# One hybrid decoder layer on one core: the first three-part product of each column block in 512 columns instead of twice 256

## The chip, the core and the metric

The kernel runs on one core of a Trainium2 chip. The metric is the device time of one execution in microseconds (us). The kernel before takes 1066.27 us, the median of three runs (1066.21, 1066.27 and 1082.69). The profile comes from a fourth execution, which took 1077.18 us. A difference of less than 2% (21.3 us of the median) is treated as no difference.

## The reference, cut to what matters

The layer has 512 tokens of width 1024 and works in float32. Three sub-layers follow each other: a SwiGLU feed-forward network (FFN), a mixer (a gated convolution beside a sparse attention), and a second FFN. Each is preceded by a norm and added to the residual stream.

```
h = modulate(rmsnorm(x))
x = x + 0.5 * gt1 * (silu(h @ w1_gate) * (h @ w1_up)) @ w1_down     # 1024 -> 2816 -> 1024
x = x + gt2 * mixer(h)        # one input projection, attention, one output projection
x = x + 0.5 * gt3 * (silu(h @ w2_gate) * (h @ w2_up)) @ w2_down
out = rmsnorm(x) * g_final
```

Nearly all arithmetic is in these matrix products. Everything is held transposed: channels lie on the 128 partitions, the 512 tokens are the columns.

## The kernel before, in words

**Three-part products.** TensorE multiplies in a 32-bit form of less precision than float32, so each float32 operand is split into a high and a low part (`whi`, `wlo` for weights; `hhi`, `hlo` for the normed input; `ghi`, `glo` for the FFN's hidden values). One product of a 128x128 weight tile with 128x512 values is made as three: high weight by high value, high weight by low value, low weight by high value. The helper `mm3` (line 280) issues them. Each matmul first loads its 128x128 weight tile (LDWEIGHTS) and then streams the columns of values (MATMUL). Where the product is 512 columns wide, `mm3` cuts it into the two halves of `HALVES`, and issues the three parts for the left half, then the three for the right: six weight loads and six matmuls of 256 columns. Both halves add up in one 128x512 bank of PSUM, of which there are eight.

**Column blocks.** A column block is one 128x512 output tile that is summed over all its input tiles in one bank, in one go on TensorE. `start` is true at its first input tile, `stop` at its last.

- `project` (line 542) makes one block from the 8 tiles of `h`. The FFN's `main` calls it twice (gate and up) for 19 of the 22 hidden tiles of each FFN; the mixer's `fill` calls it for 14 blocks.
- `part` (line 616) makes one block of the FFN's down projection from 11 hidden tiles. `main` calls it 8 times for the first half of the hidden tiles and 8 times for the second; of the latter the last two blocks are made in separate 256-column halves.
- `output` (line 1650) makes the mixer's output projection from 8 tiles: five blocks side by side, a sixth alone, and the last two in separate halves.

The other three hidden tiles of each FFN and the mixer's first six blocks are made by `first_products` and `first_group`, which start with a 256-column half, because the operands of the two halves become ready at different times.

**Order of the work.** All instructions are written out in straight line. A planner (class `Plan`) simulates the five engines with fixed costs for every operation and so decides the order in which the instructions are put into each engine's queue. A three-part product of 512 columns has the cost `c_mm3(512)`, whatever number of instructions it is made of. Weights come by DMA in units of 512 KB; ScalarE (ACT) rounds them to `whi` (line 372) and VectorE (DVE) or GpSimd (POOL) makes `wlo` (line 361). The two last units of the first FFN and of the mixer are kept in tiles of their own (`whik`, `wlok`, and `PT`).

Of the kernel before, what the change touches and what calls it, by code (L numbers as in the profile page):

```python
# [255 lines left out]
def tile_hymba_layer(ctx: ExitStack, tc: tile.TileContext, xT, pos, cols_d, con_d, wa0, wa1, f1a, f1b, f1d,  # L256
# [9 lines left out]
    HALVES = (slice(0, T // 2), slice(T // 2, T))  # L266
# [10 lines left out]
    def mm(o, lhsT, rhs, start, stop):  # L277
        nc.tensor.matmul(o, lhsT, rhs, start=start, stop=stop)  # L278

    def mm3(o, w, x_, start, stop):  # L280

        n = o.shape[-1]
        wide = n == T and x_[0].shape[-1] == T
        halves = HALVES if wide else (slice(0, n),)
        for ts in halves:
            x0, x1 = (x_[0][:, ts], x_[1][:, ts]) if wide else x_
            o_ = o[:, ts] if wide else o
            mm(o_, w[0], x0, start and ts is halves[0], False)
            mm(o_, w[0], x1, False, False)
            mm(o_, w[1], x0, False, stop and ts is halves[-1])  # L290
# [251 lines left out]
    def project(b):  # L542

        u = take_unit()
        yield made[u]
        for d in range(DK):
            yield c_mm3(T)
            mm3(bank_of[b], cols(u, d), h_of(d), d == 0, d == DK - 1)
        free_unit(u)
# [17 lines left out]
    def first_group(order, built, accs, end, n_cols=2 * GRP):  # L567

        uses = {}
        for n, (i, d) in enumerate(order):  # L570
            yield built[i, d]
            if d not in uses:
                uses[d] = take_unit()
            yield made[uses[d]]
            ts = HALVES[i]
            for j in range(n_cols):
                if n == 0:
                    accs[j] = yield banks
                yield c_mm3(T // 2)
                mm3(bank_of[accs[j]][:, ts], cols(uses[d], j), h_of(d, ts), n == 0, n == len(order) - 1)  # L580
            if i == 1:
                free_unit(uses[d])
        done(end)


    def ffn(s, gp, accs, norm, end):
# [30 lines left out]
        def part(half, d, b, ts, keep=False):  # L617
            for k in range(FH):
                n = d * FH + k
                if (half, n // 8) not in at:  # L620
                    at[half, n // 8] = take_unit()
                u = at[half, n // 8]
                yield made[u]
                yield g_in[half * FH + k]
                yield c_mm3(ts.stop - ts.start)
                mm3(bank_of[b][:, ts], cols(u, n % 8), (ghi[k][:, ts], glo[k][:, ts]), k == 0, k == FH - 1)
                if n % 8 == 7 and not keep:
                    free_unit(u)
                if half == 0 and d == DK - 1:
                    give(gs[k], k)  # L630
# [38 lines left out]
    start = ctx.enter_context(ExitStack())  # L669
# [298 lines left out]
    with ExitStack() as mixer:  # L968
# [634 lines left out]
        n = 0  # L1603
# [295 lines left out]
```

## Time and profile before

| what | value |
|---|---|
| three runs | 1066.21, 1066.27, 1082.69 us |
| median | 1066.27 us |
| the profiled execution | 1077.18 us |
| its span, first to last instruction | 1075.4 us |
| TensorE (PE) busy | 1054.2 us, 98% |
| weight loads (PEld) busy | 1009.8 us, 94% |
| VectorE (DVE), ScalarE (ACT), GpSimd (POOL) busy | 606.0, 408.7, 51.2 us |
| matmuls, and as many weight loads | 8753 |
| mean granted TensorE clock | 0.991 of full speed |

The profiled execution has 1.8 us around its span. Matmuls are pipelined: the recorded duration of one (about 0.28 us for 256 columns) is longer than the time until the next one starts, so the busy share of TensorE says little, and the spacing of the starts tells how fast it works. A number of matmuls divided into a stretch in which TensorE does nothing else gives that spacing.

### The profile page before, as it was taken

To read this page: it belongs to the slowest core of one execution; us is meant where nothing else is said; L and a number is where in the kernel's file an instruction comes from. 1 tells how busy PE (TensorE), PEld (TensorE's weight loads), DVE (VectorE), ACT (ScalarE), POOL (GpSimd) and SP (SyncE) were. 2 spreads that over 40 slices of the span, in tenths; PEclk is the share of its full clock that TensorE was granted. 3 is DMA by queue.
4 is the path that set the end of the run, shared out by engine and by line. 5 is a ranking of instruction groups with operands and counts; after the bars stand their busy time and mean duration, and the time that the engine had idled before them with its cause. 6 is when DMAs were issued, how large, how long until landed. Compare 5 with 4: busy or idle time off the path is not lost.

```text
span 1075.4 us, 20561 instructions
## 1 busy us (share of the span) xinstructions
PE 1054.2 (98%) x8753; PEld 1009.8 (94%) x8753; DVE 606.0 (56%) x1069; ACT 408.7 (38%) x713; POOL 51.2 (5%) x47
## 2 busy tenths in 40 slices
PE   8999999999999999999999999999999999999997
PEld 5899999999999999998887789999999999999997
DVE  4988888833333347699787786744333333233334
ACT  4552222222222224458566775333222122222321
POOL 0310100000000001021001010000000000000000
PEclk8999999999999999999999999999999999999999
DMA  9669999422232231344201014133233322322202
GB/s 336 250 217 324 326 322 323 150 99 99 99 99 99 93 89 48 122 125 160 80 18 37 1 29 130 45 118 118 83 95 99 98 84 94 99 99 85 93 21 79
DMA packets 40732, 134.02 MB, mean 125 GB/s; under 512 B 4704, under 2 KB 8032, under 8 KB 40000
## 3 DMA queue, kind: packets, MB, share of 16 engines
q1 hardware_dynamic: 40640, 132.71, 37.0%
q8 instruction: 68, 1.11, 0.4%
q14 instruction: 24, 0.20, 0.1%
HBM read 130.14 MB, written 2.10 MB: 123 GB/s over the span
## 4 chain that ended last, share of the span: by engine, by line
PE 80%; DVE 10%; DMA 6%; issue 2%; ACT 1%; SPq 0%; DVEq 0%; ACTq 0%
PE b L278 77%; DMA araw<-in_wa_dram 6%; DVE ada L871 3%; PE b L1402 2%; DVE wlo L361 2%; DVE afirst L742 1%; DMA wfirst<-in_wa_dram 1%; DVE glo L613 1%; DVE s L525 1%; ACT whi L372 0%; PE b L1297 0%; DVE s L1045 0%; DVE s L606 0%; DVE swp L1048 0%; DVE afirst L739 0%
## 5 line engine op out<-in xcount | busy, mean ns | idle before, releaser
L278 PE MATMUL b<-hhi,whi 128*128 128x256 f32 x1824 | 515.8, 283 | 0.0
L278 PE MATMUL b<-hlo,whi 128*128 128x256 f32 x1824 | 509.2, 279 | 0.6 <-DVE hlo L531 0.6
L278 PE MATMUL b<-hhi,wlo 128*128 128x256 f32 x1824 | 508.7, 279 | 0.0
L372 ACT ACTIVATE whi<-raw 128x1024 fp32r<-128x1024 f32 (+3 forms) x176 | 178.2, 1013 | 461.4 <-issue 250.3
L278 PEld LDWEIGHTS b<-hhi,whi 128*128 128x128 f32 x1824 | 343.3, 188 | 7.6 <-issue 6.7
L278 PEld LDWEIGHTS b<-hlo,whi 128*128 128x128 f32 x1824 | 346.5, 190 | 1.1 <-DVE hlo L531 1.0
L278 PEld LDWEIGHTS b<-hhi,wlo 128*128 128x128 f32 x1824 | 343.5, 188 | 0.0
L361 DVE TENSOR_TENSOR wlo<-raw,whi 128x1024 fp32r<-128x1024 f32 (+3 forms) x162 | 191.1, 1180 | 223.8 <-ACT whi L372 223.5
L278 PE MATMUL b<-ghi,whi 128*128 128x256 f32 x672 | 188.0, 280 | 0.0
L278 PE MATMUL b<-ghi,wlo 128*128 128x256 f32 x672 | 187.3, 279 | 0.0
L278 PE MATMUL b<-glo,whi 128*128 128x256 f32 x672 | 187.3, 279 | 0.0
L278 PEld LDWEIGHTS b<-glo,whi 128*128 128x128 f32 x672 | 127.6, 190 | 0.0
L278 PEld LDWEIGHTS b<-ghi,whi 128*128 128x128 f32 x672 | 126.2, 188 | 0.8 <-issue 0.8
L278 PEld LDWEIGHTS b<-ghi,wlo 128*128 128x128 f32 x672 | 126.3, 188 | 0.0
L606 DVE TENSOR_TENSOR s<-sg,b 128x512 f32<-128x512 f32 x44 | 30.0, 685 | 102.1 <-PE b L278 101.4
L871 DVE SCALAR_TENSOR_TENSOR ada<-araw,cact,ada 128x1024 f32<-128x1024 f32 x49 | 63.5, 1296 | 16.8 <-DMA araw<-in_wa_dram 16.2
L361 POOL TENSOR_TENSOR wlo<-raw,whi 128x768 fp32r<-128x768 f32 (+2 forms) x14 | 32.2, 2299 | 213.5 <-ACT whi L372 213.5
L538 DVE SCALAR_TENSOR_TENSOR x<-b,mod,x 128x512 f32<-128x512 f32 (+1 forms) x30 | 19.1, 643 | 40.8 <-PE b L278 40.7
L456 ACT ACTIVATE s<-x 128x256 f32<-128x256 f32 (+1 forms) x41 | 19.4, 491 | 54.8 <-DVE x L538 52.8
L611 ACT ACTIVATE ghi<-s 128x512 fp32r<-128x512 f32 x44 | 27.1, 620 | 15.5 <-DVE s L606 15.5
L529 ACT ACTIVATE hhi<-s,mod 128x256 fp32r<-128x256 f32 (+1 forms) x42 | 20.9, 534 | 31.2 <-DVE s L525 25.6
L613 DVE TENSOR_TENSOR glo<-s,ghi 128x512 fp32r<-128x512 f32 x44 | 32.1, 734 | 0.0
(238 smaller groups left out, 963.7 us busy)
## 6 DMA issues: line engine op xcount, KB each, us to landing
araw<-in_wa_dram SPq DMA_DIRECT2D x56, 512.0 KB
raw<-in_f1b_dram SPq DMA_DIRECT2D x38, 512.0 KB
raw<-in_f2b_dram SPq DMA_DIRECT2D x38, 512.0 KB
raw<-in_f1d_dram SPq DMA_DIRECT2D x22, 512.0 KB
raw<-in_f2d_dram SPq DMA_DIRECT2D x22, 512.0 KB
raw<-in_wib_dram SPq DMA_DIRECT2D x14, 512.0 KB
wfirst<-in_wa_dram SPq DMA_DIRECT2D x5, 1024.0 KB
raw<-in_wc_dram SPq DMA_DIRECT2D x8, 512.0 KB
```

The source lines that it names most:

```text
L278: nc.tensor.matmul(o, lhsT, rhs, start=start, stop=stop)
L361: (nc.vector if e == DVE else nc.gpsimd).tensor_sub(wlo_of[j][:, :n], raw_of[i][:, :n], whi_of[j][:, :n].bitcast(F32))
L372: nc.scalar.activation(whi_of[j][:, :n], raw_of[raw_at[u]][:, :n], AF.Copy)
L456: nc.scalar.activation(o[:, ts], x[d][:, ts], AF.Square)
L525: nc.vector.scalar_tensor_tensor(t, x[d][:, ts], am[:, s, d:d + 1], rb(), op0=OP.mult, op1=OP.mult)
L529: nc.scalar.activation(hhi[d][:, ts], t, AF.Identity, bias=sh)
L538: nc.vector.scalar_tensor_tensor(x[d][:, ts], bank_of[b][:, ts], gate, x[d][:, ts], op0=OP.mult, op1=OP.add)
L606: nc.vector.tensor_mul(scr_of[q], sg_of[k], bank_of[bu])
L611: nc.scalar.activation(ghi[j], scr_of[q], AF.Copy)
L613: nc.vector.tensor_sub(glo[j], scr_of[q], ghi[j].bitcast(F32))
L871: nc.vector.scalar_tensor_tensor(a, w, cact[:, k:k + 1], a, op0=OP.mult, op1=OP.add)
L1402: nc.tensor.transpose(pt[:, w:w + P], Pr[t][:, kb * P:(kb + 1) * P], ident)
```

## The change

`mm3` no longer cuts a 512-column product into halves where `start` is true. The first input tile of each column block is then made in three matmuls of 512 columns, with three weight loads; all later tiles of the block stay in six matmuls of 256 columns.

```
     def mm3(o, w, x_, start, stop):
 
+
         n = o.shape[-1]
         wide = n == T and x_[0].shape[-1] == T
-        halves = HALVES if wide else (slice(0, n),)
+        halves = HALVES if wide and not start else (slice(0, n),)
         for ts in halves:
             x0, x1 = (x_[0][:, ts], x_[1][:, ts]) if wide else x_
             o_ = o[:, ts] if wide else o
```

The planner's costs, the order of the work, the DMAs and the other engines' instructions are the same.

## Rows read from the trace of the kernel before

**Rows 1.** The page: busy us, share of the span and instructions of each engine.

```profile
PE 1054.2 (98%) x8753; PEld 1009.8 (94%) x8753; DVE 606.0 (56%) x1069; ACT 408.7 (38%) x713; POOL 51.2 (5%) x47
```

**Rows 2.** The page: the chain that ended last, by engine.

```profile
PE 80%; DVE 10%; DMA 6%; issue 2%; ACT 1%; SPq 0%; DVEq 0%; ACTq 0%
```

**Rows 3.** Matmuls by form: shapes, count | busy us, mean ns | idle before.

```profile
L278 PE MATMUL b<-hlo,whi 128*128 128x256 f32 x1824 | 509.2, 279 | 0.6 <-DVE hlo L531 0.6
```

**Rows 4.** Windows: us, busy (instructions) PE, PEld, DVE, ACT, POOL, granted clock, DMA share, GB/s.

```profile
200.00:390.00 190.00, 190.00 (x1679) 190.00 (x1678) 74.37 (x85) 54.03 (x67) 0.00 (x0) 1.00 0.30 100
700.00:1050.00 350.00, 350.00 (x2975) 350.00 (x2973) 121.36 (x135) 97.81 (x124) 0.00 (x0) 1.00 0.29 91
...
43.00:46.00 3.00, 3.00 (x16) 3.00 (x15) 3.00 (x5) 0.85 (x2) 2.07 (x1) 0.50 0.02 8
```

**Rows 5.** Timeline of PE near 198 us: start us, us, instruction, count.

```profile
197.99 0.37 PE L278 MATMUL b<-ghi,whi 128*128 128x256 f32 x1
198.19 0.28 PE L278 MATMUL b<-glo,whi 128*128 128x256 f32 x1
...
198.43 0.28 PE L278 MATMUL b<-ghi,whi 128*128 128x256 f32 x1
...
198.77 0.28 PE L278 MATMUL b<-ghi,whi 128*128 128x256 f32 x1
```

**Rows 6.** Timeline of PE near 696 us, columns the same.

```profile
696.11 0.36 PE L278 MATMUL b<-hhi,whi 128*128 128x256 f32 x1
696.31 0.28 PE L278 MATMUL b<-hlo,whi 128*128 128x256 f32 x1
...
696.90 0.28 PE L278 MATMUL b<-hhi,whi 128*128 128x256 f32 x1
```

**Rows 7.** Timeline of PE: the attention's 512-column matmuls, twice.

```profile
577.33 0.62 PE L278 MATMUL b<-PT,V 128*128 128x512 f32 x2
577.79 0.49 PE L1402 MATMUL b<-con,P 128*128 128x128 f32 x3
...
641.80 0.62 PE L278 MATMUL b<-PT,V 128*128 128x512 f32 x2
642.26 0.27 PE L1402 MATMUL b<-con,stab 128*128 128x128 f32 x1
```

**Rows 8.** Timeline of PE from 44.76 to 47.19 us.

```profile
44.76 0.41 PE L278 MATMUL b<-hlo,whi 128*128 128x256 f32 x1
...
45.83 0.41 PE L278 MATMUL b<-hhi,whi 128*128 128x256 f32 x1
...
46.36 0.28 PE L278 MATMUL b<-hhi,whi 128*128 128x256 f32 x1
...
47.19 0.28 PE L278 MATMUL b<-hlo,whi 128*128 128x256 f32 x1
```

**Rows 9.** Timeline of PE: 256-column matmuls behind wider ones, at two places.

```profile
455.96 0.29 PE L278 MATMUL b<-whi,hlo 128*128 128x280 f32 x1
456.08 0.28 PE L278 MATMUL b<-hhi,whi 128*128 128x256 f32 x1
...
456.56 0.28 PE L278 MATMUL b<-hlo,whi 128*128 128x256 f32 x1
...
456.90 0.28 PE L278 MATMUL b<-hlo,whi 128*128 128x256 f32 x1
...
554.90 0.59 PE L278 MATMUL b<-PT,V 128*128 128x384 f32 x2
555.33 0.28 PE L278 MATMUL b<-hhi,whi 128*128 128x256 f32 x1
...
556.50 0.28 PE L278 MATMUL b<-hlo,whi 128*128 128x256 f32 x1
```

**Rows 10.** Windows of two larger stages, columns as in Rows 4.

```profile
50.00:198.00 148.00, 142.09 (x1249) 137.31 (x1248) 124.73 (x134) 46.28 (x67) 9.84 (x5) 1.00 0.84 294
...
413.00:690.00 277.00, 276.01 (x2096) 244.46 (x2096) 217.02 (x541) 169.49 (x364) 28.20 (x24) 1.00 0.25 77
```

More of the change, by code (lines that the diff above doesn't have):

```diff
@@ L283, in mm3 @@
         wide = n == T and x_[0].shape[-1] == T
-        halves = HALVES if wide else (slice(0, n),)
+        halves = HALVES if wide and not start else (slice(0, n),)
         for ts in halves:
```

## The prediction

> **What bounds the kernel now.** The page of the profile comes first. TensorE is busy for 98% of the span, VectorE for 56%, ScalarE for 38% [rows 1]. The chain that ended last runs over TensorE for 80% of the time [rows 2]. So TensorE sets the end almost everywhere, and what counts is how closely its matmuls follow each other. The groups by form are led by the 256-column parts of the three-part product, with hardly any idle time in front (0.6 us in all for the 1824 parts with `hlo`) [rows 3].
>
> Then I asked for two long windows in which TensorE does nothing else, and divided. 190 us hold 1679 matmuls, two or three of which only reach in from the left: 190/1677 is 113.3 ns from start to start. In the second FFN 350 us hold 2975: 350/2972 is 117.8 ns [rows 4]. Same code, same shapes, same clock (1.00), and 4.4 ns (3.9%) apart. So there are two paces, a short one and a long one. The timeline shows when a pace is taken: in the first few matmuls after an interruption. Near 198 us the first start is followed by the second after 0.20 us, two more come in 0.24 us, then three in 0.34 us, and 113.3 ns holds from there through the window up to 390 us [rows 4, 5]. Near 696 us it begins alike with 0.20 us, but the next five take 0.59 us, 118 ns each, and the long pace holds to 1050 us [rows 4, 6]. Neither stretch leaves its pace by itself.
>
> **What the change removes and adds.** In each FFN `project` makes 2 x 19 blocks and `part` 8 + 6 full ones: 52, for two FFNs 104. The mixer adds 14 by `project` and 6 in `output`. That is 124 blocks, and in each six 256-column matmuls become three of 512: 372 matmuls and 372 weight loads fewer, of 8753 [rows 1]. The columns streamed are the same.
>
> - **The price of a 512-column matmul.** It replaces two starts, 2 x 113.3 = 226.7 ns at the short pace or 235.6 ns at the long. The nearest rows are the attention's 512-column matmuls: two take 577.79 - 577.33 = 0.46 us, and again 642.26 - 641.80 = 0.46, so 230 ns each [rows 7]. The bound from below is the columns alone. Up to 46 us the granted clock is 0.50 [rows 4], and there five starts take 1.07 us: 214 ns for 256 columns, one column per cycle of 1.2 GHz [rows 8]. At full clock twice the columns would take the same 214 ns at least (an estimate from this row). The bound from above is 237 ns, the 230 and one rounding step of both rows. I take 230, the same kind of operand and width. At the short pace that is 372 x 3.3 = 1.2 us lost, at the long one 372 x 5.6 = 2.1 us won; the bounds give from 372 x 12.7 = 4.7 won to 372 x 10.3 = 3.8 lost, and at the long pace from 8.0 won to 0.5 lost. With either pace, this term is small.
> - **The weight loads** that go were under the matmuls: nothing but the pace itself shows them.
> - **Operands and order.** A 512-column first part needs all columns of `h` or `g` at once. They are written 512 wide, or (after `first_group`) both halves have long been written. The low value is needed one 512-column part in, later than before, when it was needed after 256; the low weight likewise. No wait is added, and nothing is queued behind one. The planner's cost is the same, so no other instruction and no DMA moves, on any queue. Nothing there costs or gains.
> - **The pace.** This is the large term. Every block now begins with three wide parts, and 42 or 60 narrow ones follow (7 tiles of 6, or 10). A wide part takes about twice as long, so the next weight load has time to spare. At each of the 124 places the pace can be taken anew. What would follow in the second FFN: at the short pace the 350 us would be 350 x 113.3/117.8 = 336.6, 13.4 us less [rows 4]. The mixer, 277 us with interruptions, shows both paces [rows 9, 10]; if half of the matmul time there is long, short would save some 3 us; I take 2.
>
> **Sum, against the profiled execution.** If the short pace comes everywhere: 1077.18 - 13.4 - 2 + 1.2 = 1063 us. The profiled execution is 10.9 us above the median, the third run 16.4. Pieces of 13.4 (second FFN) and 7.5 (the 190 us, if long) are of that size, so I think it likelier (6 in 10) that the median is an execution whose second FFN fell into the short pace, and that a profile costs little. Then 1063 stands as it is, about 3 us under the median. If instead profiling cost the 10.9, everything moves down by it, to 1052.
>
> **Forecast: the short pace nearly everywhere.** For it: 4.4 ns is a misfit of load and stream in the long pace that never heals when undisturbed, and one row shows the hand-over from wider parts healing it: behind the last 280-column part four narrow ones take 0.48 us (120 ns each), the next three 0.34 us (113 ns) [rows 9]. And where the short pace already runs, the load still begins with each part and waits, so a longer part keeps the phase.
>
> **Rivals.**
>
> - **The pace goes on as it was.** The three wide parts are no interruption, the pace of a stretch is still fixed where the stretch begins. For it: 1677 matmuls without a change of pace in the first window, across blocks and from `h` to `g` operands [rows 4]. Against: those all had one width. Only the small term is left, about 1 us either way: 1066 us, with its bounds 1058 to 1070.
> - **The wide part runs at one column per cycle, and the pace as before.** At 214 ns instead of 230 [rows 8], 372 x 12.7 = 4.7 us are won where short, 8.0 where long: about 1061. For it: the load of a wide part is long done before the next begins. Against: the attention's 230 ns [rows 7], though these alternate two sizes of weight tile. [...]
> - **The wide part throws the stream into the long pace, block after block: slower.** The place is the hand-over from the third wide part to the first narrow one, where the weight load has been waiting. Two rows look like this. At half clock loads are hidden under 214 ns parts, and when the clock rises, seven narrow parts take 0.83 us, 119 ns each [rows 8]. Behind a 384-column part of the attention ten narrow parts take 1.17 us, 117 ns [rows 9]. Price: the 190 us at the short pace become 197.5, the same share of the 148 us before (in part hidden there, the DMA is 84% busy) and of the mixer's short half adds 4 + 4 [rows 4, 10]: 1077.18 + 15.5 - 2.1 = 1091 us, or 1080 if profiling cost the 10.9. It passes 2% over the median when some 4,800 more matmuls than in the median runs are long (21.3 us / 4.4 ns); 8381 are left.
> - **That the change doesn't do what it says** can be left aside: `start` is true for the first tile of all 124 blocks, whose products are 512 wide.
>
> **How the numbers follow.** Short nearly everywhere 0.42, pace unchanged 0.28, one column per cycle 0.10, long 0.20. The likeliest gives 1063 by the sum; the one in which profiling cost 10.9 weighs less but lies below, and with the cheaper wide part the sum falls by up to 6 us; I keep 1062. Its own range is 1050 to 1067. The range for all reaches down to 1049 (short, with the profile's cost) and up to 1083, which takes in the long case at 1080 but not at 1091 (0.2 x 0.6 = 0.12 left out, and some 0.05 below). What can be told from no change is 2%, below 1044.9 or above 1087.6. Faster: short everywhere with the cheapest wide part and the whole 10.9 of the profile, 1066.27 - 15.4 - 4.7 = 1046, doesn't quite reach it: 0.04. Slower: the long case at 1091, 0.11. Within: 0.85.
>
> **What would show it.** In the profile after: 8381 matmuls; 124 x 3 matmuls of 128x512 in the groups of line 278 for `hhi,whi`, `hlo,whi` and their like. The spacing of their starts tells 214 from 230 and 237. The windows of 200 to 390 and 700 to 1050 us hold the pace: 113.3 ns between the narrow parts in both would be my forecast, 117.8 in both the slower rival, one of each the unchanged pace. The timeline just behind a wide part shows whether the spacing is settled there anew. The forecast is wrong if the pace within one block differs from that of the next without an interruption, or if the wide parts cost well over 237 ns.

## The result, and the profile after

The change makes the kernel slower: 1078.08 us median of four runs (1075.50 to 1080.07, the highest with a profile) against 1066.76 for the kernel before, 11.3 us, a ratio of 1.0106 (95% interval 1.0076 to 1.0137). That is clear of no change, though under the 2% that counts as a difference here. Medians are over all runs; ratios leave out, as a slower state, runs more than 1.5% above the fastest of their kernel. The forecast was 4 us faster. The time lies in the range, on the wrong side.

The page of the changed kernel, the rows that answer to [rows 1, 2]:

```profile
span 1078.3 us, 19817 instructions
...
PE 1056.1 (98%) x8381; PEld 996.6 (92%) x8381; DVE 606.2 (56%) x1069; ACT 409.0 (38%) x713; POOL 50.0 (5%) x47
...
PE 84%; DMA 7%; DVE 6%; issue 1%; ACT 0%; SPq 0%; DVEq 0%; ACTq 0%
```

8381 matmuls and as many weight loads, 372 fewer, as counted. TensorE has even more of the chain. The groups by form (count | busy us, mean ns | idle before) have 96 wide parts of each kind on `h`:

```profile
L278 PE MATMUL b<-hlo,whi 128*128 128x256 f32 x1632 | 457.6, 280 | 0.6 <-DVE hlo L532 0.6
...
L278 PE MATMUL b<-hhi,whi 128*128 128x512 f32 x96 | 38.1, 397 | 0.0
L278 PE MATMUL b<-hlo,whi 128*128 128x512 f32 x96 | 38.0, 395 | 0.0
L278 PE MATMUL b<-hhi,wlo 128*128 128x512 f32 x96 | 38.0, 395 | 0.0
```

No idle time has appeared in these groups, and in the whole span TensorE is idle for 1078.3 - 1056.1 = 22.2 us, against 21.2 before. So the lost time is in the spacing of the starts. The timeline of TensorE around three groups of wide parts, one block after the other in the first FFN (start us, recorded duration us):

```profile
298.90 0.28 PE L278 MATMUL b<-hhi,wlo 128*128 128x256 f32 x1
299.01 0.39 PE L278 MATMUL b<-hhi,whi 128*128 128x512 f32 x1
299.24 0.40 PE L278 MATMUL b<-hlo,whi 128*128 128x512 f32 x1
299.47 0.39 PE L278 MATMUL b<-hhi,wlo 128*128 128x512 f32 x1
299.70 0.28 PE L278 MATMUL b<-hhi,whi 128*128 128x256 f32 x1
...
304.53 0.28 PE L278 MATMUL b<-hhi,wlo 128*128 128x256 f32 x1
304.65 0.39 PE L278 MATMUL b<-hhi,whi 128*128 128x512 f32 x1
304.88 0.39 PE L278 MATMUL b<-hlo,whi 128*128 128x512 f32 x1
305.11 0.40 PE L278 MATMUL b<-hhi,wlo 128*128 128x512 f32 x1
305.34 0.28 PE L278 MATMUL b<-hhi,whi 128*128 128x256 f32 x1
...
310.11 0.39 PE L278 MATMUL b<-hhi,whi 128*128 128x512 f32 x1
```

Between the first and the second group lie 42 narrow parts in 304.65 - 299.70 = 4.95 us, 117.9 ns each: long. Between the second and the third lie another 42 in 310.11 - 305.34 = 4.77 us, 113.6 ns: short. Nothing but the wide parts stands between them, and each group takes 0.69 us. **The pace has flipped at each group.** Read to the nanosecond, the starts in the trace do so from block to block: of the groups between two readable stretches (ten spacings or more on either side, not counting the first five behind the group), all 52 behind a short stretch are followed by a long one, and all 51 behind a long stretch by a short one. Behind short parts the three wide ones take 226, 236 and 230 ns, 692 in all, where six short narrow ones take 680; behind long parts mostly 231, 229 and 236, 696, where six long ones take 707. So the wide parts cost nothing on balance, and half of the narrow parts are long.

That sum closes. The 124 blocks keep 96 x 42 + 28 x 60 = 5,712 narrow parts; half of them at 4.44 ns more is 12.7 us over a kernel that is short throughout. Measured are 11.3 over the median, whose runs aren't short throughout either. The traces give the sum directly as well. Added up over all narrow parts that follow a narrow one (spacings over 125 ns, thus interruptions, left out), the time beyond 113.3 ns is 17.5 us in the changed kernel. In the profiled kernel before, with its long second FFN, it is 17.6; in a profiled execution of nearly the same kernel with a short second FFN (e9 below) it is 6.2, which is 11.3 less than in the changed one.

### The profile page after: what moved, and what is told of

Same layout as the page of the kernel before. It is cut to its first block, busy times and chain, and to the rows that moved or that the text cites. A ratio compares the mean times of both kernels' runs of the same rounds, so it can differ in the third digit from the quotient of the medians.

```text
span 1078.3 us, 19817 instructions
## 1 busy us (share of the span) xinstructions
PE 1056.1 (98%) x8381; PEld 996.6 (92%) x8381; DVE 606.2 (56%) x1069; ACT 409.0 (38%) x713; POOL 50.0 (5%) x47
## 4 chain that ended last, share of the span: by engine, by line
PE 84%; DMA 7%; DVE 6%; issue 1%; ACT 0%; SPq 0%; DVEq 0%; ACTq 0%
PE b L278 81%; DMA araw<-in_wa_dram 6%; DVE ada L872 3%; PE b L1403 2%; DMA wfirst<-in_wa_dram 1%; DVE wlo L362 1%; DVE afirst L743 1%; DVE s L526 0%; DMA raw<-in_f1b_dram 0%; PE b L1298 0%; DVE glo L614 0%; DVE s L607 0%; DVE afirst L740 0%; DVE v L400 0%; DVE afirst L735 0%
## 5 line engine op out<-in xcount | busy, mean ns | idle before, releaser
L278 PE MATMUL b<-hhi,whi 128*128 128x256 f32 (+1 forms) x1728 | 501.8, 290 | 0.0
L278 PE MATMUL b<-hlo,whi 128*128 128x256 f32 (+1 forms) x1728 | 495.5, 287 | 0.6 <-DVE hlo L532 0.6
L278 PE MATMUL b<-hhi,wlo 128*128 128x256 f32 (+1 forms) x1728 | 495.0, 286 | 0.0
L278 PEld LDWEIGHTS b<-hhi,whi 128*128 128x128 f32 x1728 | 326.1, 189 | 11.6 <-issue 6.7
L278 PEld LDWEIGHTS b<-hlo,whi 128*128 128x128 f32 x1728 | 329.1, 190 | 5.1 <-DVE hlo L532 1.0
L278 PEld LDWEIGHTS b<-hhi,wlo 128*128 128x128 f32 x1728 | 326.7, 189 | 3.7
L278 PE MATMUL b<-ghi,whi 128*128 128x256 f32 (+1 forms) x644 | 183.6, 285 | 0.0
L278 PE MATMUL b<-ghi,wlo 128*128 128x256 f32 (+1 forms) x644 | 183.0, 284 | 0.0
L278 PE MATMUL b<-glo,whi 128*128 128x256 f32 (+1 forms) x644 | 183.0, 284 | 0.0
L1414 DVE TENSOR_TENSOR PT<-b,PT 128x384 fp32r<-128x384 f32 (+1 forms) x48 | 28.2, 598 | 5.1 <-ACT PT L1412 4.5
```

What stands on the lines that cost most here:

```text
L1414: nc.vector.tensor_sub(pl[:, :w], pt[:, :w], ph[:, :w].bitcast(F32))
```

## The experiments

The theory under test is the flip: three wide parts turn the short pace into the long one and back. Where a diff names `seen[0]`, it is a counter of the 512-column blocks begun so far (1 to 52 the first FFN, 53 to 72 the mixer, 73 to 124 the second FFN), `seen[1]` the number of the tile in its block.

**e1, the kernel before again**, without an edit.

> The kernel before once more, for a second look at its paces. Theory (a group of three wide parts flips the pace, so that half the narrow parts of the changed kernel are long, while the kernel before keeps the pace with which a stretch begins): every long stretch is at one pace throughout, 113.3 or 117.8 ns from start to start, but which one may differ from the first profile; with the second FFN at the short pace the execution takes 1062 to 1068 us, with it long 1075 to 1079. Rival (profiling itself costs the 10.9 us): the second FFN is long again and the profiled execution is at 1077, while the runs without a profile stay at 1066 to 1067.

1081.73 us profiled, beside 1068.04 for a run without a profile. Windows in the first and the second FFN, columns as in [rows 4]:

```profile
200.00:390.00 190.00, 190.00 (x1678) 190.00 (x1678) 75.93 (x90) 54.03 (x66) 0.00 (x0) 1.00 0.30 100
704.00:1050.00 346.00, 346.00 (x2940) 346.00 (x2939) 121.19 (x135) 97.80 (x124) 0.00 (x0) 1.00 0.29 92
```

Again short in the first (190/1676 = 113.4 ns) and long in the second (346/2937 = 117.8), each unbroken. This looked like the rival, by which the profile has the cost; e5 decides between them.

**e2, every second block.**

```
+        halves = HALVES if wide and not (start and seen[0] % 2) else (slice(0, n),)
```

> Only every second column block begins with 512-column parts (62 blocks instead of 124). Theory of the flip: the pace changes at each of these blocks and nowhere else in between, so two blocks short are followed by two blocks long; half of the narrow parts are long as in the changed kernel, 1074 to 1080 us. Rival (the pace belongs to the place: gate blocks long, up blocks short): all narrow parts of the FFNs take the pace that the blocks with wide parts had, all long (about 1088) or all short (about 1063). Rival (the wide parts themselves cost the time): half the loss, about 1072, whatever the paces.

1075.75 us. Four windows that follow each other, each holding the narrow parts between two groups, now 90 over two blocks:

```profile
263.60:273.60 10.00, 10.00 (x91) 10.00 (x90) 3.20 (x4) 2.45 (x4) 0.00 (x0) 1.00 0.32 106
274.50:284.90 10.40, 10.40 (x91) 10.40 (x90) 3.20 (x4) 2.45 (x4) 0.00 (x0) 1.00 0.30 102
285.80:295.80 10.00, 10.00 (x91) 10.00 (x90) 3.19 (x4) 2.44 (x4) 0.00 (x0) 1.00 0.30 105
296.70:307.10 10.40, 10.40 (x91) 10.40 (x90) 3.19 (x4) 2.45 (x4) 0.00 (x0) 1.00 0.30 102
```

Windows of 10.0 and 10.4 us hold the same 91 matmuls in turn. The pace passes the border of an unchanged block and flips at the next changed one, which among the blocks of `project` is always a gate block or always an up block. So it is not the place that chooses. Half the groups leave as much time in long starts as all of them: 17.7 us beyond 113.3 ns a start, against the 17.5 above. The time itself, of one run, lies in the theory's 1074 to 1080; with 1072 from the rival by which the wide parts cost it, the windows decide.

**e3, two tiles**, six wide parts in a row.

```
+        halves = HALVES if wide and seen[1] > 1 else (slice(0, n),)
```

> The first two tiles of each block in 512 columns, six wide parts in a row instead of three. Theory of the flip: three wide parts flip, six flip twice, so a stretch keeps the pace with which it begins, over its block borders; with wide parts at 231 ns six of them cost 26 ns more than 12 short narrow ones, 3 us in all. Time near that of the kernel before plus 3: 1069 where stretches begin short. Rival (every hand-over from a wide to a narrow part flips, however many wide ones went ahead): short and long blocks alternate as in the changed kernel, about 1078.

1070.61 us in one run, with twice as many wide parts as in the changed kernel and 7.5 less than its median. Two stretches that follow each other in the first FFN, between the last wide part of a group and the first of the next:

```profile
265.91 0.40 PE L278 MATMUL b<-hhi,wlo 128*128 128x512 f32 x1
266.14 0.28 PE L278 MATMUL b<-hhi,whi 128*128 128x256 f32 x1
...
270.23 0.39 PE L278 MATMUL b<-hhi,whi 128*128 128x512 f32 x1
...
271.62 0.28 PE L278 MATMUL b<-hhi,whi 128*128 128x256 f32 x1
...
275.71 0.39 PE L278 MATMUL b<-hhi,whi 128*128 128x512 f32 x1
```

Both hold 36 narrow parts in 4.09 us, 113.6 ns each. Read to the nanosecond, all 97 groups behind a short stretch are followed by a short one. A group of six does not flip; the rival (any hand-over flips) falls.

**e4, other numbers and another place.**

```
+        kind = seen[0] % 3 if wide else 0
+        if kind and start:
+            mm(o, w[0], x_[0], True, False)
+            if kind == 2:
+                mm(o, w[0], x_[1], False, False)
...
+            return
+        halves = HALVES if wide and (kind or not stop) else (slice(0, n),)
```

> Three kinds of blocks in turn: the first tile with one wide part (high by high) and four narrow; the first tile with two wide parts and two narrow; no wide part at the first tile but three at the last, so that the hand-over lies between two blocks. Meant as a table of hand-overs: which pace follows on which. Theory of the flip, if it is a matter of the phase between weight load and column stream and not of where in a block the parts stand: the three wide parts at the last tile flip as those at the first do; one or two wide parts shift the phase by other amounts and may keep the pace, flip it or set it to one value. Rival (start of a bank's sum matters): no flip behind the last tile. Time between 1062 and 1080, by the share of long blocks.

1069.76 us. The three wide parts at a block's end were joined by the one at the start of the next block, so they made groups of four, which the expectation had not foreseen. A group of four and one of two, in the second FFN:

```profile
761.05 0.28 PE L278 MATMUL b<-hhi,wlo 128*128 128x256 f32 x1
761.16 0.39 PE L278 MATMUL b<-hhi,whi 128*128 128x512 f32 x1
...
762.09 0.28 PE L278 MATMUL b<-hlo,whi 128*128 128x256 f32 x1
...
767.31 0.39 PE L278 MATMUL b<-hhi,whi 128*128 128x512 f32 x1
767.54 0.40 PE L278 MATMUL b<-hlo,whi 128*128 128x512 f32 x1
```

From the first narrow part behind the four (762.09) to the two (767.31) lie 46 narrow parts in 5.22 us, 113.5 ns: short as before them. So wide parts at the start of a bank's sum do not flip by standing there: groups of two and of four include that start and leave short short. Nor is it a wide part with the low weight that flips, since the groups of four hold one as the groups of three do. Whether three at a block's end alone would flip was left untested. All nine profiles that have both wide parts and stretches of narrow ones give a table (groups between readable stretches as defined above, without the kept weight units; read to the nanosecond):

```
wide parts   behind short: short / long    behind long: short / long
2            165 / 0                       7 / 3
3            0 / 80                        75 / 0
4            32 / 0                        1 / 2
6            97 / 0                        1 / 3
```

Behind short parts wide ones take 226, 236, 231, 236, 231, 236 ns; the narrow parts go on short behind a 236 and long behind a 231, hence the parity. Of the odd numbers only three has more than one case behind short parts; the one group of nineteen (where `output` holds five blocks open) turned short into long too. Long parts have a cycle of three: any three starts in a row take 353 or 354 ns together. Behind them an even group's outcome depends on where in that cycle it is met: two wide parts of 231 and 229 stay long, of 233 and 234 (either way round, within 1 ns) end short. A group of three ended short in both of these cases, 71 times as 231, 229, 236 (within 1 ns) and 4 times as 233, 233, 234 (in any order).

**e5, one group of three in the whole kernel**, at block 73.

```
+        halves = HALVES if wide and not (start and seen[0] == 73) else (slice(0, n),)
```

> One single group of three wide parts in the whole kernel: at the first block that `project` makes in the second FFN. Theory (three wide parts flip the pace; the second FFN is long when profiled and short in the runs of the kernel before at 1066 to 1068): profiled, the second FFN enters long and is flipped to short at this block, and the execution takes about 13 us less than the profiled kernel before, 1064 to 1068; the runs without a profile enter short, are flipped to long and get 13 us slower, 1079 to 1081. Rival (profiling costs 11 us by itself and the second FFN is long in all executions): all get faster by 13, the runs without a profile come to 1053 to 1055. Rival (the wide parts cost the time): no change, three parts cost 12 ns.

1078.93 us median, ratio 1.0092 (1.0054 to 1.0129): **one group, three matmuls of 8750, costs as much as the 124 of the change.** This profiled execution entered the second FFN short. The windows before and behind the group:

```profile
700.00:723.00 23.00, 23.00 (x205) 23.00 (x204) 9.51 (x14) 8.53 (x11) 0.00 (x0) 1.00 0.39 119
724.00:1040.00 316.00, 316.00 (x2685) 316.00 (x2685) 108.14 (x116) 85.65 (x109) 0.00 (x0) 1.00 0.29 91
```

113 ns (23/203), then 117.8 (316/2683) for the rest of the FFN. The entry of the profiled kernel was forecast wrongly, the mechanism rightly: the runs without a profile came to 1076 to 1084, around the theory's 1079 to 1081, where the rival has 1053 to 1055. So most runs of the kernel before must have a short second FFN (worked out from these times; a run without a profile has no trace), and the 10.9 us of the first profile were its pace, not the price of profiling.

**e6, all wide.**

```
-        wide = n == T and x_[0].shape[-1] == T
-        halves = HALVES if wide else (slice(0, n),)
-        for ts in halves:
...
+        mm(o, w[0], x_[0], start, False)
+        mm(o, w[0], x_[1], False, False)
+        mm(o, w[1], x_[0], False, stop)
```

> No product is cut into halves: every 512-column product is three wide parts. The price of a wide part with no narrow ones between, and no pace of narrow parts to choose. Theory (wide parts behind wide parts alternate between 231 and 236 ns, 233.4 on average, as in the six-part groups): 3,228 wide parts cost 6.7 ns more than two short narrow ones each, 22 us in all over a kernel that is short everywhere (1060), so 1080 to 1086. Rival (230 ns as first taken): 11 us, about 1071. Rival (213 to 216 ns once nothing disturbs): about 1020 to 1030.

1083.23 us in one run, within the theory's 1080 to 1086 (the trace has 3,336 wide parts rather than 3,228, which adds 0.7 us to its sum). A window in the first FFN:

```profile
200.00:390.00 190.00, 190.00 (x817) 153.10 (x816) 74.92 (x89) 52.79 (x64) 0.00 (x0) 1.00 0.29 96
```

190/815 = 233 ns for 512 columns, against 226.7 for two short narrow parts. The weight loads are busy for 153 us of 190 and have time to spare, and that does not help.

**e7, two wide parts at every block**, with the two low-by-high parts narrow.

```
+        if wide and start:
+            mm(o, w[0], x_[0], True, False)
+            mm(o, w[0], x_[1], False, False)
+            for ts in HALVES:
+                mm(o[:, ts], w[1], x_[0][:, ts], False, False)
+            return
+        halves = HALVES if wide else (slice(0, n),)
```

> Each block begins with two wide parts (high by high, high by low) and two narrow ones (low by high), an even number in place of three. Theory (behind short narrow parts wide ones take 226, 236, 231, 236, 231, ... ns in turn, and the narrow parts go on short behind a 236 and long behind a 231): two wide parts keep the short pace, and where a stretch begins long, its blocks of 44 and 62 narrow parts (no multiple of three) reach the wide parts at another point of the long pace's cycle of three each time, until one of them ends short. So nearly all is short, in every execution: 1061 to 1066 us, 1 to 5 below the kernel before. Rival (any hand-over flips): half long, 1075 to 1080. Rival (each hand-over costs some 13 ns and the long pace is kept where it is met): 1067 to 1082 as before.

1068.99 us, ratio 0.9998 (0.9971 to 1.0026), runs from 1066.16 to 1072.33. The loss of the change is gone, with 124 groups of wide parts left in. The paces are as expected: 100 groups behind short stay short. Where a stretch began long, at 458.6 us, the first group (230, 230 ns) left it long, the second (233, 234) set it short:

```profile
463.28 0.28 PE L278 MATMUL b<-hlo,whi 128*128 128x256 f32 x1
...
464.22 0.39 PE L278 MATMUL b<-hhi,whi 128*128 128x512 f32 x1
464.46 0.39 PE L278 MATMUL b<-hlo,whi 128*128 128x512 f32 x1
...
465.27 0.28 PE L278 MATMUL b<-hhi,whi 128*128 128x256 f32 x1
...
466.18 0.28 PE L278 MATMUL b<-hhi,wlo 128*128 128x256 f32 x1
```

Eight in 0.94 us before it (117.5 ns), eight in 0.91 behind it (113.8). The forecast of 1061 to 1066 was too low: what I took for a kernel short throughout (1060) can't be had, since in the trace 15 of the mixer's 34 stretches of eight or more parts are long, and the kept weight units of the first FFN and the mixer run at 119 to 120 ns; in all, 4.8 us beyond 113.3 ns a start are left.

**e8, two wide parts at some blocks.**

```
+        if wide and start and (seen[0] <= 28 or 52 < seen[0] <= 78):
```

> The same two wide parts, but only where stretches are interrupted often or begin: the first 28 blocks of the first FFN, the mixer's 20, and the first six `project` blocks of the second FFN; the other 70 blocks narrow throughout, as in the kernel before. Theory: the pace is set short by the last such block and then kept, so it costs less than two wide parts everywhere by 70 x 13 ns = 1 us: 1060 to 1065 us. Rival (the short pace is lost without being set anew): near the kernel before, 1066 to 1082.

1066.89 us, ratio 0.9981 (0.9953 to 1.0009): not clear of no change, 2 us above what was expected. Its profiled execution entered the second FFN long (29 us hold 249 matmuls, 117.9 ns) and was short behind the six blocks (286 us hold 2526, 113.3 ns).

**e9, two groups of three**, at blocks 73 and 74.

```
+        halves = HALVES if wide and not (start and 73 <= seen[0] <= 74) else (slice(0, n),)
```

> Two groups of three wide parts in the whole kernel: at the first and at the second block that `project` makes in the second FFN (e5 had the first alone). Theory of the flip: the second group takes back what the first did after one block, so an execution that enters the second FFN short is short again from the second block on: as the kernel before, 1066 to 1069 us and a ratio of 1.000, against the 1.009 of one group. Rival (wide parts, or a hand-over, leave something behind that costs time): as one group or worse, a ratio of 1.009 to 1.02.

The profiled execution took 1066.82 us. Windows before the first group, between the two, and behind the second:

```profile
702.00:726.00 24.00, 24.00 (x215) 24.00 (x214) 10.50 (x18) 8.89 (x13) 0.00 (x0) 1.00 0.37 111
727.60:732.20 4.60, 4.60 (x42) 4.60 (x41) 4.31 (x6) 3.06 (x6) 0.00 (x0) 1.00 0.59 169
734.00:1040.00 306.00, 306.00 (x2702) 306.00 (x2701) 105.86 (x114) 83.54 (x105) 0.00 (x0) 1.00 0.29 90
```

113 ns, 115 to 118 (too short a window to count better; the starts give 117.8), then 306/2700 = 113.3: flipped, and flipped back. The times don't settle it: 1064.78 and 1066.82, but also 1082.38 and 1089.82, while the kernel before spread from 1062.62 to 1090.58 beside it. The trace alone counts here. It shows one thing more: with a profile and a short second FFN the execution takes 1066.82 us, so profiling itself costs little.

**e10, two wide parts at six blocks of the second FFN.**

```
+        if wide and start and 73 <= seen[0] <= 78:
```

> Two wide parts (an even number) at the first six `project` blocks of the second FFN, all else as in the kernel before. Theory: executions that enter the second FFN short stay so, those that enter long are set short within the first blocks; the cost is 6 x 13 ns. The typical run stays at 1065 to 1068, the long ones of the kernel before (1074 to 1080) no longer occur for this reason: a mean 0.1 to 0.3% lower, a ratio of 0.997 to 0.999. Rival (the runs of the kernel before at 1074 and above have another cause): they occur here too, ratio 1.000.

1068.28 us against 1070.09, ratio 0.9997 (0.9974 to 1.0019): no gain in the ratio. Its twelve runs lie between 1065.54 and 1070.26; of 17 of the kernel before on that chip six took 1075 or more. Were the two kernels alike, twelve runs without any of these would come about once in forty times (an estimate from these counts). The profiled execution shows the repair, in a second FFN that was entered long:

```profile
704.00:729.00 25.00, 25.00 (x214) 25.00 (x213) 10.60 (x18) 9.05 (x13) 0.00 (x0) 1.00 0.36 108
...
758.00:1040.00 282.00, 282.00 (x2491) 282.00 (x2490) 97.53 (x103) 76.93 (x96) 0.00 (x0) 1.00 0.30 91
```

25/212 = 118 ns before the first group, 282/2489 = 113.3 behind the last. That the runs at 1075 and above are those that enter long fits this, but runs without a profile have no trace, so it isn't shown run by run. And e5 fits it less well: of all runs of the kernel before about a quarter took 1074 or more (12 of 47), and such an entry would have been flipped to short there, yet none of its nine runs without a profile came below 1076. Of the five profiled executions that are the same up to that point (before, e1, e5, e9, e10), three entered long; whether a profile makes that likelier is open.

## Why the prediction was wrong

- **What bounds the kernel** held: TensorE's starts, in two paces that keep themselves, and whatever the change costs shows in them alone.
- **The count** (372 fewer of each) and **the price of a wide part** (230 ns) held: 692 and 696 ns for three in place, 233 each in e6. The bounds of 214 and 237 held the measured 233, and the rival of one column per cycle is out. The Trainium skill's page "TensorE: Matmul & The Clock Gate" gives, in its section on the back-to-back issue gap, a formula for an isolated matmul by which 512 columns would take 215.8 ns (an estimate: 512 over 2.4 GHz, plus 2.5 ns); in this stream, with a weight load for each part, they take 233.
- **Operands, order, other engines** held: 22.2 us of idle time against 21.2.
- **The size of the pace** held (13.4 us for the second FFN long or short): e5 lost 10.8 us over the last 316 of its 350 us, for which the same step gives 11.9.
- **Which execution the median is**, given 6 in 10, came out as taken: its second FFN is short (by the times of e5 and the profiled time of e9; no run without a profile shows it directly).
- **The forecast step failed**: "the short pace nearly everywhere", because a wide interruption heals the long pace, and where the short pace runs "a longer part keeps the phase". The first half is right: a group of three ends every long stretch. The second is wrong: the same group ends every short stretch (80 of 80). So the sum's largest term, 13.4 + 2 us won by the pace, came out as a loss of about 11: half of the narrow parts long, where the kernel before has most of them short in its typical run. The rows behind 280 and 384 columns [rows 9] had one hand-over each, from different states, and I read from them a preference of wide parts where only a dependence on the state before could be had. No rival had the flip; the slower one ("block after block" long) was half of it, and its 1091 and 1080 both lie above 1078. That the time lies in the range at all is luck: the range was carried up to 1083 for that rival.
- What the forecast lacked was a second step: if the outcome depends on the phase at which a group is met, a group that repeats identically must be followed through twice. A map that takes short to long and long to short gives half and half, whatever the start. Why three wide parts do that inside the chip stays open.

## What to carry to other kernels

When a stream of equal instructions shows two self-keeping paces, ask of a change not which pace it brings but what it does to each of them; a disturbance that repeats once per block can flip at each. Count the disturbances by parity, and prefer a form that leaves the good pace alone (here two wide parts, not three, though two gained nothing over none). And before pricing against a profile, find out which pace that execution had: here it lay 11 us from the median.

## What was not expected of the hardware

- With 32-bit operands and a fresh 128x128 weight load for each part, matmuls of 256 columns follow each other every 113.3 or every 117.8 ns at the granted clock of 1.00, and each spacing keeps itself, over 2,745 matmuls and more, on the same code and data. What the two differ in inside the chip stays open: no run here shows it. In the trace of the kernel before, read to the nanosecond, a weight load starts about 3 ns after a matmul in both, and the next matmul starts 110 ns after that in the short pace and 114 to 115 in the long.
- 512 columns take 233 ns (e6), more than two of 256 at the short pace (226.7) and less than two at the long one (235.6), though the weight loads then have slack.
- One group of three wide matmuls moved the whole kernel by 0.9%, where it stood ahead of some 2,800 equal narrow parts (e5).
